# Two-layer decoder trunk on one core: an order from deadlines for four engines, and kept sums in 2 KB tiles

## The chip, the cores and the metric

The kernel runs on one core of a Trainium2 chip. A core has a matrix engine (PE, with its weight loads PEld), a vector engine (DVE), a scalar engine (ACT), GpSimd (POOL), and a queue processor (SP) that only issues transfers; ACT and POOL issue transfers too. Each engine works through its own list of instructions in the order in which they stand in the built program, and an instruction waits there on semaphores for what it needs. The metric is the device time of one execution in microseconds, as the median over several runs.

## The reference

The trunk has two layers over 256 positions and a model width of 2048, in float32, with a batch of one. Cut to what matters:

```python
h = rms_norm(x, mix_norm[l])
q, k, v, uv, gate_logits = split(h @ w_in[l])                 # 2048 x 7680
branch_a = sliding_window_attention(rope(norm(q)), rope(norm(k)), v, sinks[l]) @ w_attn_branch[l]
branch_b = chunked_sgu(gelu(uv), w_spatial[l], ...) @ w_sgu_branch[l]
gates = sigmoid(gate_logits)
merged = gates[..., :D] * branch_a + gates[..., D:] * branch_b
x = x + merged @ w_out[l]
h2 = rms_norm(x, ffn_norm[l])
x = x + (silu(h2 @ w_gate[l]) * (h2 @ w_up[l])) @ w_down[l]   # 2048 x 5632 and back
```

Attention has 16 query heads and 4 key heads of 64 and a window of 128; the gating unit mixes chunks of 128 positions in 8 groups. Nearly all the arithmetic is in the matrix products with the weights, which are read from HBM once.

## The kernel before

**Products.** Every weight matrix is cut into pieces of 256 rows by 512 columns (512 KB). Such a piece is an *entry*. It is loaded into a `raw` tile by a transfer on SP (L235), and split into a high part `whi` (a rounded copy on ACT, L261) and a low part `wlo` (`raw - whi` on DVE, L262). The activations are split in the same way into `uh` and `ul`. PE adds three products for each pair of blocks: `whi*uh`, `wlo*uh`, `whi*ul` (L361 and L362). An ordinary entry is 12 matmuls of 512 columns for both halves of the 256 positions.

Two column blocks that meet the same activations form a pair plan. In its head one or two units of four weight blocks are multiplied in Winograd's form with seven products in place of eight: DVE forms differences of weight blocks in place (L246), and of activation blocks (`sums`, `sh`, `sl`: L520 and L506, or L546 and L552 for a second unit). The head's entries, P1 to P7, are 6 matmuls each. ACT keeps one partial sum aside in `kept` (P5, L384), DVE adds to it (L387), and ACT writes it back into PSUM (L390). `kept` is one tile of 4 KB per partition from the pool `big` (31 slots).

**Order of PE.** PE's order is written out by hand: entries of a plan, with the head of the next plan woven into the end of the plan before. It is a manual schedule in both kernels.

**Order of the other engines.** The code asks for work at *slots*. A slot is passed each time an ordinary entry's worth of matmuls has been written, and `after(n, fn)` puts a step `n` slots ahead; `n` is a table of numbers set by hand (`WINO_NORM`, `SCORES`, `V_STEP` and so on, L28 to L58). Loads are asked for 7 entries ahead (`W_LOAD`), splits 4 ahead (`W_SPLIT`), weight differences 6 ahead (`W_SUM`). Steps are tied with `tc.issue_after` to the newest `wlo`, `whi` or load on their own engine, as here (L280 to L288):

```python
    def tick():
        slot_no[0] += 1
        due = [s for s in steps if s[0] <= slot_no[0]]
        steps[:] = [s for s in steps if s[0] > slot_no[0]]
        for _, fn in sorted(due, key=lambda s: s[0]):
            with tc.issue_after(stream.last.ins):
                fn()
```

The framework's scheduler then makes one list per engine from these ties and its own timeline.

**Pools.** `raw` tiles have 5 buffers, `whi` and `wlo` 4 each, `tmp` (tag `t2`, 2 KB per partition) 4, PSUM accumulators 4 and two times 2 smaller sets. `tmp` holds squares, attention scores (`pr`) and spatial weights. A feed-forward layer runs in three rounds of 4, 4 and 3 column blocks of 512. After each of the first two, `chunk` (L961 to L965) copies each result from PSUM into a 4 KB tile `part` of `big` and adds it to `held_x` in DRAM by one accumulating transfer of 512 KB from POOL. Transposes go through DVE (`box`, L431) and 16 transfers of 32 KB each (`gather`, L437), on SP, POOL or both.

Of the kernel before, what the change touches and what calls it, by code (L numbers as in the profile page):

```python
# [1 line left out]

# [6 lines left out]
F32 = mybir.dt.float32  # L9
# [3 lines left out]
AX = mybir.AxisListType  # L13

# [47 lines left out]

@with_exitstack
def hybrid_trunk(ctx: ExitStack, tc: tile.TileContext, x, mix_norm, w_in, q_norm, k_norm, sinks,
# [155 lines left out]
    class Stream:  # L220
# [7 lines left out]
        def load(self, upto):  # L228
            while self.asked < min(upto, len(entries)):
                for key, w, h, tag in entries[self.asked]["loads"]:  # L230
                    raw = (slot([P, 2, CW], name="raw") if tag == "slot" else
                           wraw.tile([P, 2, CW], F32, tag=tag, name=nm("raw"), bufs=None if tag == "raw" else 1))
                    for dst, src in rows_of(raw, w, h):
                        if self.raws:
                            self.loaded = nc.sync.dma_start(dst, src)  # L235
                        else:
                            for i in range(2):
                                self.loaded = nc.sync.dma_start(dst[:, i:i + 1], src[:, i:i + 1])
# [3 lines left out]
        def add(self, upto):  # L242
            while self.summed < min(upto, len(entries)):
                for d, x, y in entries[self.summed].get("sums", ()):
                    with tc.issue_after(self.last.ins):
                        self.last = nc.vector.tensor_tensor(out=self.raws[d], in0=self.raws[x], in1=self.raws[y],  # L246
                                                            op=ALU.subtract)
                self.summed += 1

        def split(self, upto):  # L250
            while len(self.parts) < min(upto, len(entries)):
# [5 lines left out]
                for i in ([slice(0, 1), slice(1, 2)] if one else [slice(0, 2)]):  # L257
                    if not self.parts and i.start == 0:
                        nc.vector.tensor_copy(hi[:, i, :], raw[:, i, :])
                    else:  # L260
                        self.high = nc.scalar.activation(hi[:, i, :], raw[:, i, :], AF.Copy)  # L261
                    self.last = nc.vector.tensor_tensor(out=lo[:, i, :], in0=raw[:, i, :], in1=hi[:, i, :].bitcast(F32),  # L262
                                            op=ALU.subtract)
# [18 lines left out]
    def tick():  # L282
# [38 lines left out]
    held = const.tile([P, 1], F32, name="held")  # L321
    hold = nc.gpsimd.tensor_copy(held, xs[2][:, 1, :1])

    def later(dst, src):
        with tc.issue_after(hold.ins):
            nc.gpsimd.dma_start(dst, src)
# [37 lines left out]
    def step():  # L364
# [17 lines left out]
        elif tag == "P5":  # L382
            p.kept = slot([P, 2, CW], name="kept")
            nc.scalar.activation(p.kept[:, 1, :], a[0], AF.Copy)  # L384
            nc.scalar.activation(a[0], a[1], AF.Copy)
        elif tag in ("P6", "P7"):
            nc.vector.tensor_tensor(out=p.kept[:, int(tag == "P7"), :], in0=a[1], in1=p.kept[:, 1, :], op=ALU.add)  # L387
        if "then" in e:
            for t, ps in enumerate(banks(p, "b")):
                nc.scalar.activation(ps, p.kept[:, t, :], AF.Copy)  # L390
# [208 lines left out]
    def squared(c):  # L599
        with tc.issue_after(stream.high.ins):  # L600
            norm.squares(c)

    for c in range(NCH):
        after(3 + c, lambda c=c: squared(c))
# [41 lines left out]
    class Layer:  # L646
# [493 lines left out]
```

## Time and profile before

| | |
|---|---|
| median of 3 runs | 2420.3 us (2419.92 to 2421.76) |
| span of the profiled execution, first to last instruction | 2416.4 us |
| the profiled execution's own time | not recorded; the median is 3.9 us over its span |
| busy: PE, PEld, DVE, ACT, POOL | 2405.1, 1970.7, 2092.0, 1532.4, 303.4 us |
| granted TensorE clock, mean | 1.000 |
| HBM read and written | 483.66 and 16.78 MB |
| transfer queues of SP and POOL | 63.6% and 6.2% of 16 engines' span |

The page of the profile lists busy time per engine, busy share in 40 slices, transfer queues, the chain of work that ended last, and the costliest groups of instructions. A line in a group or a timeline reads: line, engine, operation, tile written `<-` tiles read, shape, count, and in brackets the idle time of the engine just before, with what ended it. Matmuls overlap: each shows about 0.39 us, but they start 0.227 us apart when nothing is late.

### The profile page before, as it was taken

The numbers are of one execution on the slowest core, as the hardware profiler recorded it, in microseconds if no ns is written. First come the engines' busy times: TensorE is split into PE (matmuls) and PEld (weight loads), VectorE is DVE, ScalarE is ACT, GpSimd is POOL, SyncE is SP. The second block draws the span as 40 slices with busy tenths as digits, with TensorE's granted clock in tenths as the row PEclk, the third lists the DMA queues.
The fourth block names the chain that finished last, engine by engine and source line by source line (L and its number), as shares of the span: only waits on it lengthen the run. The fifth ranks groups of instructions, "written<-read, shape, count | busy, mean of one in ns | idle before, by whom it ended". The sixth has DMA issues, their size and how long they took to land.

```text
span 2416.4 us, 31069 instructions
## 1 busy us (share of the span) xinstructions
PE 2405.1 (100%) x10692; PEld 1970.7 (82%) x10692; DVE 2092.0 (87%) x2409; ACT 1532.4 (63%) x1932; POOL 303.4 (13%) x557
## 2 busy tenths in 40 slices
PE   9999999999999999999999999999999999999999
PEld 7877888888888888888888778888888888888887
DVE  7779787898999998799887897878889989998998
ACT  6477555576666675666665775555676666666665
POOL 1100001132110111001301000011311101110010
PEclk9999999999999999999999999999999999999999
DMA  8755678687677757776957557776867786677773
GB/s 287 233 167 164 178 204 251 221 264 239 191 238 228 239 179 223 245 225 178 293 177 260 174 160 197 215 223 227 269 219 232 213 258 204 199 231 229 235 223 138
DMA packets 285070, 527.16 MB, mean 218 GB/s; under 512 B 28208, under 2 KB 40080, under 8 KB 284912
## 3 DMA queue, kind: packets, MB, share of 16 engines
q1 hardware_dynamic: 263056, 486.36, 63.6%
q0 software_dynamic: 21536, 38.56, 6.2%
q8 instruction: 83, 1.36, 0.2%
q14 instruction: 75, 0.61, 0.1%
q10 hardware_dynamic: 320, 0.27, 0.0%
HBM read 483.66 MB, written 16.78 MB: 207 GB/s over the span
## 4 chain that ended last, share of the span: by engine, by line
PE 88%; DVE 4%; DMA 4%; issue 1%; ACT 1%; SPq 1%; POOL 0%; DVEq 0%; ACTq 0%
PE acc L361 58%; PE acc L362 29%; DVE wlo L262 2%; DMA raw<-in_w_up_dram 2%; DMA raw<-in_w_in_dram 1%; DMA tt<-box 1%; ACT whi L261 1%; DVE raw L246 1%; SPq L437 1%; PE psc L807 1%; PE po L859 0%; PE psg L942 0%; PE ppt L844 0%; PE pt L474 0%; POOL tt L437 0%
## 5 line engine op out<-in xcount | busy, mean ns | idle before, releaser
L261 ACT ACTIVATE whi<-raw 128x1024 fp32r<-128x1024 f32 (+1 forms) x1116 | 1166.6, 1058 | 786.3 <-PE acc L362 440.0
L262 DVE TENSOR_TENSOR wlo<-raw,whi 128x1024 fp32r<-128x1024 f32 (+1 forms) x1117 | 1343.5, 1216 | 269.3 <-ACT whi L261 255.3
L361 PE MATMUL acc<-whi,uh 128*128 128x512 f32 x2854 | 1116.7, 391 | 1.4 <-ACT uh L460 1.4
L361 PE MATMUL acc<-wlo,uh 128*128 128x512 f32 x2854 | 1113.3, 390 | 2.1 <-DVE wlo L262 1.3
L362 PE MATMUL acc<-whi,ul 128*128 128x512 f32 x2854 | 1112.1, 390 | 0.6 <-DVE ul L465 0.6
L361 PEld LDWEIGHTS acc<-wlo,uh 128*128 128x128 f32 x2854 | 536.0, 188 | 118.5 <-DVE wlo L262 6.6
L361 PEld LDWEIGHTS acc<-whi,uh 128*128 128x128 f32 x2854 | 535.9, 188 | 117.8 <-issue 4.9
L362 PEld LDWEIGHTS acc<-whi,ul 128*128 128x128 f32 x2854 | 535.9, 188 | 112.8 <-DVE ul L465 1.5
L437 POOL DMA_DIRECT2D tt<-box x464 | 228.0, 499 | 1202.6 <-DVE box L431 339.7
L246 DVE TENSOR_TENSOR raw<-raw,raw 128x1024 f32<-128x1024 f32 x292 | 355.5, 1218 | 5.2 <-DMA raw<-in_w_up_dram 2.9
L361 PE MATMUL acc<-wlo,sh 128*128 128x512 f32 x584 | 228.1, 391 | 2.0 <-DVE wlo L262 2.0
L361 PE MATMUL acc<-whi,sh 128*128 128x512 f32 x584 | 228.4, 391 | 0.0
L362 PE MATMUL acc<-whi,sl 128*128 128x512 f32 x584 | 227.5, 390 | 0.0
L361 PEld LDWEIGHTS acc<-wlo,sh 128*128 128x128 f32 x584 | 109.7, 188 | 26.3 <-DVE wlo L262 4.1
L361 PEld LDWEIGHTS acc<-whi,sh 128*128 128x128 f32 x584 | 109.7, 188 | 25.1 <-issue 2.3
L362 PEld LDWEIGHTS acc<-whi,sl 128*128 128x128 f32 x584 | 109.6, 188 | 22.7
L387 DVE TENSOR_TENSOR kept<-acc,kept 128x512 f32<-128x512 f32 x102 | 69.6, 682 | 9.3 <-PE acc L362 9.3
L390 ACT ACTIVATE acc<-kept 128x512 f32<-128x512 f32 x102 | 59.7, 588 | 2.3 <-DVE kept L387 1.0
L964 POOL DMA_DIRECT2D held_x<-part x16 | 13.9, 868 | 301.4 <-ACT part L963 301.4
L333 POOL TENSOR_TENSOR rv<-ve,neg_half 128x4 f32<-128x4 f32 x8 | 10.2, 1273 | 266.8 <-DVE ve L907 247.9
L384 ACT ACTIVATE kept<-acc 128x512 f32<-128x512 f32 x51 | 30.1, 591 | 10.8 <-PE acc L362 10.5
L829 ACT ACTIVATE pr<-pr,negm 128x128 f32<-128x128 f32 x64 | 24.9, 390 | 16.0 <-DVE negm L820 16.0
(149 smaller groups left out, 909.0 us busy)
## 6 DMA issues: line engine op xcount, KB each, us to landing
raw<-in_w_in_dram SPq DMA_DIRECT2D x239, 512.0 KB, 4.8
raw<-in_w_gate_dram SPq DMA_DIRECT2D x176, 512.0 KB, 4.6
raw<-in_w_up_dram SPq DMA_DIRECT2D x176, 512.0 KB, 5.4
raw<-in_w_down_dram SPq DMA_DIRECT2D x176, 512.0 KB, 5.3
raw<-in_w_out_dram SPq DMA_DIRECT2D x64, 512.0 KB, 6.9
raw<-in_w_attn_branch_dram SPq DMA_DIRECT2D x64, 256.0 KB, 7.0
raw<-in_w_sgu_branch_dram SPq DMA_DIRECT2D x32, 512.0 KB, 5.8
tt<-box POOLq DMA_DIRECT2D x464, 32.0 KB, 4.7
```

What stands on the lines that cost most here:

```text
L246: self.last = nc.vector.tensor_tensor(out=self.raws[d], in0=self.raws[x], in1=self.raws[y], op=ALU.subtract)
L261: self.high = nc.scalar.activation(hi[:, i, :], raw[:, i, :], AF.Copy)
L262: self.last = nc.vector.tensor_tensor(out=lo[:, i, :], in0=raw[:, i, :], in1=hi[:, i, :].bitcast(F32), op=ALU.subtract)
L361: nc.tensor.matmul(ps, a, part[:, kk, :], start=first and kk + n == 0, stop=False, skip_group_check=True)
L362: nc.tensor.matmul(ps, b, hi[:, kk, :], start=False, stop=kk == 1, skip_group_check=True)
L384: nc.scalar.activation(p.kept[:, 1, :], a[0], AF.Copy)
L387: nc.vector.tensor_tensor(out=p.kept[:, int(tag == "P7"), :], in0=a[1], in1=p.kept[:, 1, :], op=ALU.add)
L390: nc.scalar.activation(ps, p.kept[:, t, :], AF.Copy)
L437: q.dma_start(dst[j * B:(j + 1) * B, i], box[i * B:(i + 1) * B, j])
L807: nc.tensor.matmul(pscore[:, i, :nk], self.qT[pair // 4][j * HD:(j + 1) * HD, pair % 4, t * P:(t + 1) * P], self.kT[j * HD:(j + 1) * HD, : ...
L829: self.exps = nc.scalar.activation(pr4[:, h, :], pr4[:, h, :], AF.Exp, bias=nm_[:, h:h + 1], accum_out=den[:, h:h + 1])
L964: nc.gpsimd.dma_start(held_x[j], part, accum_op=ALU.add)
```

## The change

**What it does.** All `tc.issue_after` ties go. While the program is traced, every pool notes which tile has which home (`Homes`). At the end `in_order` goes over the traced instructions:

1. `works` gives each instruction a price (`Work`: a pitch for its engine, and a time to its result), and finds what it needs, who needs it, and which buffers it takes.
2. `count_back` starts from PE, whose matmuls are laid end to end, and counts back for every other instruction the latest time at which it may start (`due`). Engines and the transfer engines are each taken as one server.
3. `play` goes forward: whenever an engine is free, it takes of the instructions that are ready, and whose buffers are free, the one with the earliest `due`; a function that needs another table on ACT counts as due 4000 ns later. PE keeps its order.
4. The resulting list of each of DVE, ACT, POOL and SP is fixed by an ordering tie from each instruction to the next.

The slots still decide what is traced when, and with it the order of PE's few other matmuls. Apart from the order, two tiles change: `kept` becomes two 2 KB tiles of `tmp` (except in the `in` plans), and `part` becomes one 2 KB tile of `tmp` per half, each added to DRAM by an accumulating transfer of 256 KB. No arithmetic is added or dropped: PE has the same 10582 instructions and DVE the same 2411; POOL issues 32 accumulating transfers for 16; ACT loads a table 14 times for 10 (Exp 5 times for 3, Gelu 6 for 4).

**What moves, at three places.** The first is VectorE near 890 us, in the first layer's feed-forward part, where a plan with two Winograd units follows another. `raw<-raw` is a difference of weight blocks, `sums` and `sl` are activation differences for a plan some ten entries later. Before:

```order
L520 TENSOR_TENSOR sums_7836<-flat_7658 128x256
L262 TENSOR_TENSOR wlo_7842<-raw_7689,whi_7841 128x1024
L520 TENSOR_TENSOR sums_7836<-sums_7836,flat_7658 128x256
L262 TENSOR_TENSOR wlo_7852<-raw_7709,whi_7851 128x1024
L520 TENSOR_TENSOR sums_7836<-flat_7658 128x256
L520 TENSOR_TENSOR sums_7836<-flat_7658,sums_7836 128x256
L262 TENSOR_TENSOR wlo_7870<-raw_7447,whi_7869 128x1024
L246 TENSOR_TENSOR raw_7689<-raw_7761,raw_7689 128x1024
L262 TENSOR_TENSOR wlo_7885<-raw_7839,whi_7884 128x1024
L246 TENSOR_TENSOR raw_7709<-raw_7798,raw_7709 128x1024
L506 TENSOR_TENSOR sl_7881<-sums_7836,sh_7880 128x1024
L262 TENSOR_TENSOR wlo_7896<-raw_7689,whi_7895 128x1024
```

And now (L521 is the old L262, L506 the old L246):

```order
L521 TENSOR_TENSOR wlo_7863<-raw_7710,whi_7862 128x1024
L521 TENSOR_TENSOR wlo_7873<-raw_7730,whi_7872 128x1024
L506 TENSOR_TENSOR raw_7730<-raw_7819,raw_7730 128x1024
L506 TENSOR_TENSOR raw_7732<-raw_7819,raw_7732 128x1024
L521 TENSOR_TENSOR wlo_7891<-raw_7467,whi_7890 128x1024
L506 TENSOR_TENSOR raw_7710<-raw_7782,raw_7710 128x1024
L521 TENSOR_TENSOR wlo_7906<-raw_7860,whi_7905 128x1024
L506 TENSOR_TENSOR raw_7712<-raw_7782,raw_7712 128x1024
L521 TENSOR_TENSOR wlo_7917<-raw_7710,whi_7916 128x1024
L521 TENSOR_TENSOR wlo_7933<-raw_7730,whi_7932 128x1024
```

The four `sums` and `sl` have left this stretch: they now stand among the `wlo` of the following ten entries. The last `wlo` before (`wlo_7896`) is the last but one now (`wlo_7917`).

The second place is the queue of SP near 1257 us, at the start of the second layer: `kT` is the transposed key tile, `ln` a table for the gating unit. Before:

```order
L235 DMA raw_11029<-in_w_in_dram 128x2x512
L235 DMA raw_11060<-in_w_in_dram 128x2x512
L437 DMA kT_10831<-box_10967 32x256 x16
L669 DMA ln_11047<-in_sgu_ln_b_dram 128x1024
L235 DMA raw_11089<-in_w_in_dram 128x2x512
L235 DMA raw_11101<-in_w_in_dram 128x2x512
L235 DMA raw_11120<-in_w_in_dram 128x2x512
```

And now (L697 is the old L437, L496 the old L235):

```order
L496 DMA raw_11097<-in_w_in_dram 128x2x512
L697 DMA kT_10868<-box_11004 32x256
L924 DMA ln_11084<-in_sgu_ln_b_dram 128x1024
L697 DMA kT_10868<-box_11004 32x256 x3
L496 DMA raw_11126<-in_w_in_dram 128x2x512
L697 DMA kT_10868<-box_11004 32x256 x5
L496 DMA raw_11138<-in_w_in_dram 128x2x512
L697 DMA kT_10868<-box_11004 32x256
L496 DMA raw_11157<-in_w_in_dram 128x2x512
L697 DMA kT_10868<-box_11004 32x256 x3
L496 DMA raw_11184<-in_w_in_dram 128x2x512
L697 DMA kT_10868<-box_11004 32x256 x3
```

The 16 small transfers stood in one block; now four weight loads stand between them.

The third place is VectorE near 2366 us, in the head of the last residual; `pt` is a transposed activation block in PSUM. Before:

```order
L262 TENSOR_TENSOR wlo_20446<-raw_20392,whi_20445 128x1024
L246 TENSOR_TENSOR raw_20356<-raw_20358,raw_20356 128x1024
L552 TENSOR_TENSOR sl_20424<-sums_20323,sh_20423 128x1024
L262 TENSOR_TENSOR wlo_20487<-raw_20230,whi_20486 128x1024
L246 TENSOR_TENSOR raw_20372<-raw_20374,raw_20372 128x1024
L457 TENSOR_TENSOR ul_20467<-pt_20468,uh_20466 128x512
L457 TENSOR_TENSOR ul_20467<-pt_20475,uh_20466 128x512
L262 TENSOR_TENSOR wlo_20502<-raw_20356,whi_20501 128x1024
```

And now (L812 is the old L552, L717 the old L457):

```order
L521 TENSOR_TENSOR wlo_20519<-raw_20465,whi_20518 128x1024
L506 TENSOR_TENSOR raw_20445<-raw_20447,raw_20445 128x1024
L521 TENSOR_TENSOR wlo_20560<-raw_20302,whi_20559 128x1024
L812 TENSOR_TENSOR sl_20497<-sums_20396,sh_20496 128x1024
L521 TENSOR_TENSOR wlo_20575<-raw_20429,whi_20574 128x1024
L521 TENSOR_TENSOR wlo_20587<-raw_20445,whi_20586 128x1024
L717 TENSOR_TENSOR ul_20540<-pt_20541,uh_20539 128x512
L717 TENSOR_TENSOR ul_20540<-pt_20548,uh_20539 128x512
```

Both `ul` now stand behind two more `wlo`, and one weight difference stands ahead of this piece. At the very start, VectorE copied `first_cols` (L316) behind the cast of the first weights (L259); now the copy stands first.

**The diff,** cut to its core:

```diff
+HAND = {PE: 54, DVE: 40, ACT: 40, POOL: 80, SP: 30}
+COST_PE = {"psg": 500, "po": 450, "psc": 400}
+SWITCH = 4000
+LATE = 0
+EARLY = 40000
+SPARE = 30000
...
+class Work:
...
+        if self.engine == PE:
+            n = elements(ins.ins[0].ap[1:])
+            self.pitch = 227 if n == CW and out.startswith("acc") else COST_PE.get(out.split("_")[0], 110)
+            self.time = 390
+        elif op == "DMACopy":
...
+            serve = size / row * (9 + row * 75 / 2048) / 16
...
+            if "cce_op=AluOpType.add" in str(ins):
+                serve *= 2
+            self.dma = serve, (2200 if far else 1550) + (900 if self.engine == POOL and size > 40000 else 0)
+            self.pitch = {SP: 648, POOL: 505}.get(self.engine, 60)
+            self.time = sum(self.dma) + 50
+        elif self.engine == ACT:
+            self.pitch = 105 + n * 0.8335 + (60 if min(sizes) == 1 else 0)
+            self.time = self.pitch + 98
+        elif self.engine == DVE:
+            self.pitch = 68 + n / 0.96 + (25 if op == "StreamTranspose" else 60 if op == "TensorScalarPtr" and n == P else 0)
+            self.time = self.pitch + 81
...
+def count_back(todo):
+    at, by = 8000.0, []
+    for w in todo:
+        if w.engine == PE:
+            w.due, at = at, at + w.pitch
+        by.append(at + SPARE)
...
+    def latest(w):
+        t = w.due + w.time if w.engine == PE else by[w.k]
+        for k in w.users + w.reused:
+            t = min(t, todo[k].due - HAND[todo[k].engine])
+        for k in w.ahead:
+            t = min(t, todo[k].due + w.time)
+        return t
...
+        if w.dma:
+            t = min(-t - 50, free.get("dma", end))
+            free["dma"] = t - w.dma[0]
+            w.due = free[w.engine] = min(t - sum(w.dma), free.get(w.engine, end) - w.pitch)
+        elif w.engine != PE:
+            w.due = free[w.engine] = min(-t - w.time + w.pitch, free.get(w.engine, end)) - w.pitch
...
+def play(todo, users, homes):
...
+            ks = [k for k in waiting[e] if ready[k] <= t and (e != PE or k == turn[0]) and fits(todo[k])]
+            if not ks:
+                continue
+            w = todo[min(ks, key=lambda k: (todo[k].due + (SWITCH if todo[k].table not in (None, table) else 0), k))]
...
+            if w.dma:
+                served = max(served, at + w.dma[1]) + w.dma[0]
+                end = served + 50
+            order[e].append(w)
...
+def in_order(tc, homes, held):
+    todo, users = works(tc.nc.cur_bb.bb.instructions, homes, held)
+    count_back(todo)
+    queued = mybir.DependencyInfo(mybir.DependencyClass.NoSync, mybir.DependencyReason.DATA)
+    order = play(todo, users, homes)
+    for e in (DVE, ACT, POOL, SP):
+        for a, b in zip(order[e], order[e][1:]):
+            tc.add_manual_dep(b.ins, a.ins.name, queued, reason="in_order")
...
         for _, fn in sorted(due, key=lambda s: s[0]):
-            with tc.issue_after(stream.last.ins):
-                fn()
+            fn()
...
         elif tag == "P5":
-            p.kept = slot([P, 2, CW], name="kept")
-            nc.scalar.activation(p.kept[:, 1, :], a[0], AF.Copy)
+            if p.key[0] == "in":
+                whole = slot([P, 2, CW], name="kept")
+                p.kept = [whole[:, i, :] for i in range(2)]
+            else:
+                p.kept = [temp(name="kept") for _ in range(2)]
+            nc.scalar.activation(p.kept[1], a[0], AF.Copy)
...
             if j not in xt:
-                part = slot([P, NT, CW], name="part")
                 for t in range(NT):
-                    nc.scalar.activation(part[:, t, :], sums[t], AF.Copy)
-                nc.gpsimd.dma_start(held_x[j], part, accum_op=ALU.add)
+                    part = temp(name="part")
+                    nc.scalar.activation(part, sums[t], AF.Copy)
+                    nc.gpsimd.dma_start(held_x[j][:, t, :], part, accum_op=ALU.add)
                 return
```

More of the change, by code (lines that the diff above doesn't have):

```diff
@@ L1 @@
+from collections import deque
 from contextlib import ExitStack
+from heapq import heappop, heappush
 import concourse.bass as bass
@@ new lines, in elements, with region, overlap @@
+def elements(ap):
+    n = 1
+    for _, c in ap:
+        n *= c
+    return n
+def region(a):
+    ap, off, name = a.ap, 0, str(getattr(a, "memref", ""))
+    if getattr(a, "bass_ap", None) is not None:
+        name, off, ap = a.bass_ap.tensor.name, a.bass_ap.offset, a.bass_ap.ap
+    step = ap[0][0]
+    p, lo = (off // step, off % step) if step else (0, off)
+    return name, (p, p + ap[0][1], lo, lo + sum(s * (c - 1) for s, c in ap[1:]) + 1)
+def overlap(a, b):
+    return a[0] < b[1] and b[0] < a[1] and a[2] < b[3] and b[2] < a[3]
@@ new lines, in works, with covers @@
+def works(traced, homes, held):
+    def covers(b, x):
+        return b[0] <= x[0] and b[1] >= x[1] and b[2] <= x[2] and b[3] >= x[3]
+    todo, users, wrote, read, last = [], {}, {}, {}, {}
+    for ins in traced:
+        if ins.engine not in ENGINES or ins.opcode in ("TilePoolBoundary", "TileManualSchedule", "RegisterMove"):
+            continue
+        w = Work(len(todo), ins)
+        todo.append(w)
+        for name, b in w.operands + w.outs:
+            w.deps |= {k for k, x in wrote.get(name, ()) if overlap(b, x)}
+        for name, b in w.outs:
+            w.deps |= {k for k, x in read.get(name, ()) if overlap(b, x)}
+            if w.engine in (DVE, ACT) and (name, w.engine) in last:
+                w.deps.add(last[name, w.engine])
+        for name, b in w.outs:
+            last[name, w.engine] = w.k
+            wrote[name] = [x for x in wrote.get(name, ()) if not covers(b, x[1])] + [(w.k, b)]
+            read[name] = [x for x in read.get(name, ()) if not overlap(b, x[1])]
+        for name, b in w.operands:
+            read.setdefault(name, []).append((w.k, b))
+        for name in {name for name, _ in w.operands + w.outs if name in homes}:
+            users.setdefault(name, []).append(w.k)
+        w.deps = {k for k in w.deps if k != w.k}
+    at = {w.ins.name: w.k for w in todo}
+    for first, then in held:
+        todo[at[first.name]].ahead.add(at[then.name])
+    takers = {}
+    for name, ks in users.items():
+        todo[ks[0]].takes.append(name)
+        todo[ks[0]].ahead.update(ks[1:])
+        takers.setdefault(homes[name], []).append((ks[0], name))
+    for (_, bufs, cyclic), rows in takers.items():
+        rows.sort()
+        order = list(dict.fromkeys(k for k, _ in rows))
+        if bufs < len(rows):
+            for a, b in zip(order, order[1:]):
+                todo[a].ahead.add(b)
+        if cyclic:
+            for (_, old), (k, _) in zip(rows, rows[bufs:]):
+                todo[k].reuse |= {u for u in users[old] if u < k}
+    for w in todo:
+        w.ahead = {k for k in w.ahead if w.k not in todo[k].deps}
+        for k in w.ahead:
+            todo[k].behind.add(w.k)
+    for w in todo:
+        w.reuse -= w.deps | w.behind
+        for k in w.deps:
+            todo[k].users.append(w.k)
+        for k in w.reuse:
+            todo[k].reused.append(w.k)
+    return todo, users
```

189 lines of the change are left out of this document (137 added, 52 removed).

## The prediction

> **What bounds the kernel now.** I read the page's head first, then the groups of PE, then stretches of the span, and last the timeline where a stretch has idle PE.
>
> ```profile
> span 2416.4 us, 31069 instructions
> PE 2405.1 (100%) x10692; PEld 1970.7 (82%) x10692; DVE 2092.0 (87%) x2409; ACT 1532.4 (63%) x1932; POOL 303.4 (13%) x557
> ...
> L361 PE MATMUL acc<-wlo,uh 128*128 128x512 f32 x2854 | 1113.3, 390 | 2.1 <-DVE wlo L262 1.3 <-DVE kept L387 0.3
> L362 PE MATMUL acc<-whi,ul 128*128 128x512 f32 x2854 | 1112.1, 390 | 0.6 <-DVE ul L465 0.6
> ...
> L361 PE MATMUL acc<-wlo,sh 128*128 128x512 f32 x584 | 228.1, 391 | 2.0 <-DVE wlo L262 2.0
> ```
>
> PE is the bound: it is idle for only 11.3 us. The change leaves PE's list alone, so all that it can win is time in which PE waits. The groups show whom it waits for: nearly always DVE, for a `wlo` that comes late. The stretches show where (columns: length, then busy time and count for PE, PEld, DVE, ACT, POOL, then clock, transfer share and GB/s):
>
> ```profile
> 0.00:40.00 40.00, 36.25 (x169) 29.74 (x170) 27.79 (x76) 26.86 (x51) 9.57 (x24) 1.00 0.95 326
> 830.00:930.00 100.00, 99.46 (x437) 81.35 (x436) 95.57 (x95) 65.84 (x75) 22.95 (x47) 1.00 0.66 203
> 1140.00:1220.00 80.00, 79.70 (x356) 64.69 (x355) 67.93 (x84) 55.26 (x82) 20.14 (x40) 1.00 0.86 278
> 1220.00:1310.00 90.00, 89.32 (x398) 73.81 (x397) 72.23 (x89) 49.07 (x54) 12.37 (x7) 1.00 0.65 210
> 2035.00:2130.00 95.00, 94.46 (x415) 77.17 (x414) 92.01 (x94) 61.84 (x71) 20.69 (x43) 1.00 0.65 202
> 2130.00:2335.00 205.00, 204.94 (x904) 169.47 (x903) 185.89 (x176) 134.36 (x152) 22.05 (x42) 1.00 0.72 224
> 2335.00:2372.00 37.00, 35.45 (x160) 28.81 (x159) 35.14 (x38) 23.98 (x30) 2.15 (x4) 1.00 0.77 271
> 2372.00:2417.00 45.00, 40.47 (x179) 33.02 (x177) 34.03 (x37) 20.32 (x22) 0.00 (x0) 0.99 0.32 106
> ```
>
> 3.75 us of idle PE lie in the first 40 us. The last stretch lacks 4.5 us, of which 0.6 lie past the span's end and 3.9 are the last result's way out, behind the last matmul; no order changes that. In between six stretches lack 0.54, 0.30, 0.68, 0.54, 0.06 and 1.55, together 3.67 us. 3.75 + 3.9 + 3.67 is all of the 11.3, so PE is not idle anywhere else. In two of them DVE is busy for 96% and 97% of the time, in a third for 95%.
>
> A stall costs more than the idle time shown:
>
> ```profile
> 2367.14 0.39 PE L361 MATMUL acc<-whi,sh 128*128 128x512 f32 x1
> 2368.78 0.50 PE L361 MATMUL acc<-wlo,sh 128*128 128x512 f32 x1 [1.25 <-DVE wlo L262]
> 2369.12 0.39 PE L362 MATMUL acc<-whi,sl 128*128 128x512 f32 x1
> 2369.35 0.40 PE L361 MATMUL acc<-whi,sh 128*128 128x512 f32 x1
> ```
>
> Undelayed matmuls start 0.23 us apart (2369.12 to 2369.35). Here three starts take 1.64 and 0.34 us, 1.52 more than twice 0.23, for 1.25 idle: 0.27 on top. With that surcharge per stall, and the stalls that I count in the timeline of each stretch (3, 4, 1, 3, 1, 2), there are 1.35, 1.4, 0.95, 1.35, 0.3 and 2.1 us to win, 7.4 together. That is an estimate, and 7.4 plus a part of the start's is the ceiling of this change.
>
> **Two backlogs of DVE (830 to 930, 2035 to 2130).**
>
> ```profile
> 887.29 0.42 DVE L520 TENSOR_TENSOR sums<-flat 128x256 f32<-128x256 f32 x1
> 887.63 0.42 DVE L520 TENSOR_TENSOR sums<-flat,sums 128x256 f32<-128x256 f32 x1
> ...
> 892.50 1.22 DVE L506 TENSOR_TENSOR sl<-sums,sh 128x1024 fp32r<-128x1024 f32 x1
> 893.64 3.49 DVE L262 TENSOR_TENSOR wlo<-raw,whi 128x1024 fp32r<-128x1024 f32 x3
> ```
>
> A full-width DVE instruction takes 1.14 us start to start (892.50 to 893.64), a quarter-width one 0.34, and nothing is idle between them: PE waits since DVE has too much ahead of `wlo`. Between two given `wlo` five entries apart, the old order has five `wlo`, three weight differences, `sl` and four `sums`; the new has five `wlo` and four differences. The count of full-width ones is equal; the four quarter-width `sums` go (4 x 0.34 = 1.4 us). One entry earlier the old order has a weight difference more, 1.1. So the late `wlo` comes 2.5 us sooner, against 1.35 us of stall: all of it goes, in both layers, **2.7**. What moved back, `sums` and `sl`, now stands beside ordinary entries, whose 12 matmuls take 12 x 0.227 = 2.7 us of PE for 1.14 of DVE; that is its cover. Without it, it would cost its own 2.5 again.
>
> **The block of small transfers on SP (1220 to 1310).**
>
> ```profile
> 1256.52 0.37 SPq L235 DMA_DIRECT2D raw<-in_w_in_dram  x1
> 1257.19 11.12 SPq L437 DMA_DIRECT2D kT<-box  x16
> ...
> 1269.04 1.40 SPq L235 DMA_DIRECT2D raw<-in_w_in_dram  x3
> ...
> 1307.59 0.50 PE L361 MATMUL acc<-wlo,uh 128*128 128x512 f32 x1 [0.68 <-DVE wlo L262]
> ```
>
> From 1256.5 to 1269.0 no weight load is issued, as 16 key transfers of about 0.63 us each and one wait stand in a block. The loads behind bunch up, and PE pays at 1307.6. With four weight loads among the 16, the longest gap is five transfers, about 3.2 us. The stall goes: **1.0**. The keys themselves come later by four issues, 4 x 0.4 = 1.6 us; PE's list reads them first behind the matmul at 1307.6, some 40 us after the last was issued (1268.3).
>
> **The last residual's head (2335 to 2372).** Ahead of the `wlo` that stalls by 1.25 us the old piece holds three full-width instructions besides two `wlo`, and two half-width `ul` (0.6 each, half of 1.14): 5 x 1.14 + 2 x 0.6 = 6.9 us. The new one, from the `wlo` that answers to its first, has `wlo`, `sl`, `wlo` and one difference less: 3 x 1.14 = 3.4, of which 1.14 was only moved ahead. Net 2.3 us sooner against 1.5 of stall. The stall before it (0.3 idle, for `kept`) gains less; I take **1.9** of 2.1, bounds 1.0 and 2.1.
>
> **The start.**
>
> ```profile
> 6.85 0.43 DVE L259 CAST whi<-raw 128x512 fp32r<-128x512 f32 x1 [5.77 <-DMA raw<-in_w_in_dram]
> 7.19 0.17 DVE L316 COPY first_cols<-pf 128x16 f32<-128x16 f32 x1
> ...
> 8.33 1.13 DVE L465 SCALAR_TENSOR_TENSOR ul<-pt,first_cols,uh 128x128 fp32r<-128x128 f32 x4 [0.33 <-ACT uh L460]
> 9.37 0.68 DVE L262 TENSOR_TENSOR wlo<-raw,whi 128x512 fp32r<-128x512 f32 x1
> ...
> 5.05 1.57 PE L474 MATMUL pt<-ident,x 128*128 128x128 f32 x8
> 7.98 0.50 PE L361 MATMUL acc<-whi,uh 128*128 128x512 f32 x1 [1.35 <-ACT uh L460]
> ```
>
> The copy waits behind a cast that waits for weights until 6.85, and ACT's `uh` waits for the copy. In front of the cast the copy runs at about 5.2, `uh` when `pt` is done (6.5), and the first matmul when the cast is (7.3): 0.6 sooner; and the second `wlo` stands behind two of the four `ul` (1.04 us for four), 0.5 more. The third wait there, 0.6 for `ul` (first fence), follows DVE's and ACT's backlog and I leave it. **1.0**, bounds 0 and 1.9.
>
> **The other two stretches.** For 1140 to 1220 (transposes and four reloads of `x` at the round's end) the order shows one reload earlier and no clear relief: **0.6**, bounds 0 and 1.4. For 2130 to 2335, **0.1** of 0.3.
>
> **Added work.** `kept` and `part` in 2 KB tiles do no work more on ACT. POOL issues 16 transfers more:
>
> ```profile
> L964 POOL DMA_DIRECT2D held_x<-part x16 | 13.9, 868 | 301.4 <-ACT part L963 301.4
> SPq L235 <- DMA held_x<-part: 11.5, 3, 4.7
> held_x<-part POOLq DMA_DIRECT2D x16, 512.0 KB, 8.0
> raw<-in_w_in_dram SPq DMA_DIRECT2D x239, 512.0 KB, 4.8
> raw<-in_w_out_dram SPq DMA_DIRECT2D x64, 512.0 KB, 6.9
> L829 ACT ACT_TABLE_LOAD x3 | 3.8, 1283 | 0.1
> ACT whi L261 <- PE acc L362: 440.0, 440, 3.2
> ```
>
> 16 x 0.87 = 14 us on an engine that is 13% busy: nothing; its idle time covers it, and without that each would delay a `tt` gather by 0.87. The 31 larger slots get room: loads waited three times, 11.5 us in all, for a `part` to leave. PE is idle in no stretch with such transfers but 2130 to 2335, by 0.06, so that is worth nothing by itself. Four more table loads are 4 x 1.28 = 5.1 us of ACT, which waits 440 us for PE to free `whi` buffers (last row): hidden, 5.1 if not.
>
> [...]
>
> **The sum.** 2.7 + 1.0 + 1.9 + 1.0 + 0.6 + 0.1 = 7.3 to win. Against it I set 1.0 for new stalls (bounds 0 and 7.4, next part). Net 6.3. The durations are from one execution with a span of 2416.4, which becomes 2410.1; the median lies 3.9 above that span, so 2420.3 - 6.3 = **2414.0**.
>
> **The rivals.**
>
> *Loads just in time by too short a price.* The new order takes a weight load to land 2200 + 256 rows x 84 / 16 + 50 = 3.6 us after its issue, with no reserve (`LATE = 0`). The rows above say 4.8 in the middle, and 6.9 for `w_out`. Where it places a load or a tail of differences to be just in time, it is 1.2 us late and PE pays 1.5 with the surcharge. For it: the weight blocks of a coming head are now loaded behind ordinary loads that they preceded. Against it: ordinary loads are still issued as buffers come free, and 51 heads each have several entries of reserve. If one head in ten pays, that is 5 x 1.5 = 7.4, and the time is 2420.4: no change.
>
> *Every stall goes and none comes.* 7.4 + 1.9 = 9.3, hence 2411.0. Against it: 1140 to 1220 has stalls of three different causes.
>
> Two chunks of one pair follow each other like this:
>
> ```profile
> 742.25 0.92 POOL L964 DMA_DIRECT2D held_x<-part  x1 [25.56 <-ACT part L963]
> 750.40 0.88 POOL L964 DMA_DIRECT2D held_x<-part  x1 [7.23 <-ACT part L963]
> ```
>
> *Slower: the four tiles of `tmp`.* In the residual of a round the next plan's `kept` holds two of them and the first chunk's `part` two, until its transfers land. If the two halves land one after the other at the 8.0 us that 512 KB took, the second tile is free after 16, while the second chunk follows by 8.2 us (750.40 - 742.25); by the program four of the eight pairs are that close. ACT then stands 8 us with all splits behind it. Beyond the 3.2 us that it was ahead at most, PE pays 4.8 each, 19 in all: 2413.0 (no other new stall) + 19 = 2432. It decides from a landing of 8 + 3.2 = 11.2 us on. Against it: halves of 256 KB should not take as long as the whole each.
>
> *Table loads on the path.* All four: 2414.0 + 5.1 = 2419.1, no change that can be told. [...]
>
> That the change doesn't do what it says is excluded by the order shown: the lists did move.
>
> **How the numbers follow.** 0.2% of 2420.3 is 4.8 us, about what a measurement of this kernel tells from no change, so faster means below 2415.5. My forecast, 2412 to 2415.4, has 0.45; all stalls gone, 0.15; late loads 0.25; table loads 0.08; `tmp` 0.07. Faster is 0.45 + 0.15 = 0.60, the same 0.25 + 0.08 = 0.33, slower 0.07. The range goes from just under the ceiling's 2411.0 through the late loads' 2420.4: 2410.7 to 2421.0.
>
> **What would show it.** Right: between 830 and 930, 1220 and 1310, 2035 and 2130, and 2335 and 2372 PE is idle by 0.1 at most; the first `acc` matmul starts near 7.4; no gap of 12 us between weight loads near 1257; the whole idle time of PE is 7 or less. Wrong: ACT's `part` or `kept` groups with idle time released by `held_x` (the `tmp` rival), PE idle by `raw` transfers in heads (late loads), or the same DVE stalls at the same places.

## The result, and the profile after

| | before | after |
|---|---|---|
| median of 4 runs each | 2420.1 us (2417.4 to 2421.8) | 2453.2 us (2451.4 to 2458.2) |
| ratio, 95% interval | | 1.0142 (1.0128 to 1.0157) |
| span of the profiled execution | 2416.4 us | 2449.7 us (its own time 2451.4) |

The change makes the kernel 33 us slower. The forecast was 6 us faster, with a range up to 2421.0. Head and PE groups of the page of after (L617 and L618 are the old L361 and L362, L647 the old L387):

```profile
span 2449.7 us, 31107 instructions
PE 2417.1 (99%) x10692; PEld 1973.3 (81%) x10692; DVE 2106.4 (86%) x2409; ACT 1543.6 (63%) x1936; POOL 319.3 (13%) x573
...
L617 PE MATMUL acc<-wlo,uh 128*128 128x512 f32 x2854 | 1116.9, 391 | 17.5 <-DVE kept L647 11.0
```

PE is still the bound, but it is now idle for 32.6 us (2449.7 - 2417.1) where it was 11.3, and its busy time grew by 12 us with the same 10692 matmuls. The largest releaser is new: `kept`, an addition of 0.7 us on DVE, ended 11.0 us of PE's idle time; before, it was 0.3.

PE's list is the same in both kernels, so the start of the same matmul can be compared in the two traces. By how much each stretch is longer than before (boundaries at times of the kernel before, us; the last stretch ends at the start of the last matmul; the last column is a kernel of the experiments below):

```
stretch of before      after   prices 5500 and 4400
   0 to   40           +1.67        +0.99
  40 to  400           +0.10        +1.39
 400 to  480           +1.62        -0.05
 480 to  560          +11.69         0.00
 560 to  640           -0.05        -0.05
 640 to  700           +1.74        +0.09
 700 to  760           +2.14        +0.38
 760 to  830           -0.22        -0.12
 830 to  930           -0.76        -0.17
 930 to 1140           +0.54        -0.17
1140 to 1220           +1.30        -1.67
1220 to 1310           -0.99        -0.99
1310 to 1600           -0.16        -0.16
1600 to 1680           +1.83        -0.07
1680 to 1780           +9.64         0.00
1780 to 1900           +0.30        +0.09
1900 to 2035           +2.13        +0.48
2035 to 2130           -0.77        -0.11
2130 to 2335           +2.93        -0.27
2335 to 2372           -1.63        -2.13
2372 to the end        -0.10        -0.07
sum                   +32.96        -2.60
```

Two thirds of the loss (11.69 + 9.64) lie in two stretches for which the prediction had no term: the end of the residual after the mixing part, in each layer, where the normed activations are transposed by `box` and the gathers `tt<-box` for the first feed-forward plans. The timelines of after at the first of them, of POOL, ACT, DVE and PE (L697 issues the gather, L720 reads it, L725 reads `uh` as well):

```profile
529.37 3.94 POOL L697 DMA_DIRECT2D tt<-box  x8 [5.57 <-DVE box L691]
534.87 3.92 POOL L697 DMA_DIRECT2D tt<-box  x8 [1.56 <-DMA tt<-box]
...
543.64 1.30 ACT L720 ACTIVATE uh<-tt,vcols 128x256 fp32r<-128x256 f32 x3 [5.71 <-DMA tt<-box]
544.85 1.04 ACT L520 ACTIVATE whi<-raw 128x1024 fp32r<-128x1024 f32 x1
...
537.21 2.35 DVE L521 TENSOR_TENSOR wlo<-raw,whi 128x1024 fp32r<-128x1024 f32 x2
544.18 1.67 DVE L725 SCALAR_TENSOR_TENSOR ul<-tt,vcols,uh 128x128 fp32r<-128x128 f32 x6 [4.62 <-ACT uh L720]
545.76 0.68 DVE L647 TENSOR_TENSOR kept<-acc,kept 128x512 f32<-128x512 f32 x1
...
541.61 0.39 PE L618 MATMUL acc<-whi,ul 128*128 128x512 f32 x1
546.50 0.80 PE L617 MATMUL acc<-wlo,uh 128*128 128x512 f32 x1 [4.50 <-DVE kept L647]
547.10 0.63 PE L617 MATMUL acc<-whi,uh 128*128 128x512 f32 x1
547.52 0.63 PE L618 MATMUL acc<-whi,ul 128*128 128x512 f32 x1
```

Read it from below. PE waits 4.5 us for `kept`. `kept` stands in DVE's list behind six `ul`, which wait for `uh` from ACT; ACT's `uh` waits 5.71 us for transfers, the last of which POOL issued at 538.3 (end of its last row less one issue of 0.5). `uh` started at 543.6, 5.3 us later. `kept` itself lacked nothing, and a `whi` behind `uh` on ACT lacked nothing either: they stood in a queue. Then PE runs 13 matmuls 0.43 us apart (547.10 to 547.52) in place of 0.23. The second layer has the same chain (ACT, then PE):

```profile
1761.00 1.31 ACT L720 ACTIVATE uh<-tt,vcols 128x256 fp32r<-128x256 f32 x3 [4.61 <-DMA tt<-box]
...
1763.86 0.50 PE L617 MATMUL acc<-wlo,uh 128*128 128x512 f32 x1 [3.45 <-DVE kept L647]
```

The kernel before at the same place: the gather is issued in one go, and its reader on ACT comes 11 us after the last issue and waits for nothing.

```profile
520.86 7.83 POOL L437 DMA_DIRECT2D tt<-box  x16 [6.61 <-DVE box L431]
...
539.67 1.70 ACT L460 ACTIVATE uh<-tt,vcols 128x256 fp32r<-128x256 f32 x4
```

The waits of ACT for gathers over the whole span (us in total, times, longest), after and then before:

```profile
ACT uh L716 <- DMA tt<-box: 27.8, 9, 5.8
ACT uh L720 <- DMA tt<-box: 27.5, 6, 6.9
ACT flat L761 <- DMA tt<-box: 22.0, 5, 6.9
ACT qT L1045 <- DMA tt<-box: 11.5, 4, 5.4
```

```profile
ACT qT L791 <- DMA tt<-box: 14.7, 4, 5.8
ACT uh L456 <- DMA tt<-box: 2.1, 2, 1.7
```

88.8 us against 16.8 in these rows. What a gather costs, and what the planner thinks, differ. The gathers that POOL issues in after, with the median from issue to landing:

```profile
tt<-box POOLq DMA_DIRECT2D x464, 32.0 KB, 4.7
```

The planner takes 32 rows of 1 KB at 46.5 ns, over 16 engines, 93 ns; with its fixed 1550 and 50 that is 1.7 us, 3.0 too short. The price isn't far from what a gather took while fewer other transfers ran. The gather of the kernel before above (520 to 529 us, DMA share 0.46) and that of after (529 to 539, DMA share 0.78), median from issue to landing:

```profile
tt<-box POOLq DMA_DIRECT2D x16, 32.0 KB, 1.7
```

```profile
tt<-box POOLq DMA_DIRECT2D x16, 32.0 KB, 4.3
```

### The profile page after: what moved, and what is told of

It is laid out like the page before. It is cut to its first block, busy times and chain, and to the rows that moved or that the text cites. A ratio compares the mean times of both kernels' runs of the same rounds, so it can differ in the third digit from the quotient of the medians.

```text
span 2449.7 us, 31107 instructions
## 1 busy us (share of the span) xinstructions
PE 2417.1 (99%) x10692; PEld 1973.3 (81%) x10692; DVE 2106.4 (86%) x2409; ACT 1543.6 (63%) x1936; POOL 319.3 (13%) x573
## 4 chain that ended last, share of the span: by engine, by line
PE 56%; DVE 7%; DMA 6%; issue 3%; ACT 1%; POOL 1%; SPq 0%; ACTq 0%; DVEq 0%; POOLq 0%
PE acc L617 37%; PE acc L618 18%; DVE wlo L521 4%; DMA tt<-box 2%; DMA raw<-in_w_down_dram 2%; ACT whi L520 1%; DVE raw L506 1%; DMA raw<-in_w_up_dram 1%; POOL tt L697 1%; DMA raw<-in_w_out_dram 0%; DMA held_x<-part 0%; DVE box L691 0%; PE psc L1061 0%; DVE hid L1327 0%; DMA held_x<-x 0%
## 5 line engine op out<-in xcount | busy, mean ns | idle before, releaser
L521 DVE TENSOR_TENSOR wlo<-raw,whi 128x1024 fp32r<-128x1024 f32 (+1 forms) x1117 | 1337.9, 1217 | 241.7 <-ACT whi L520 234.9
L617 PE MATMUL acc<-wlo,uh 128*128 128x512 f32 x2854 | 1116.9, 391 | 17.5 <-DVE kept L647 11.0
L617 PE MATMUL acc<-whi,uh 128*128 128x512 f32 x2854 | 1118.9, 392 | 0.1
L618 PE MATMUL acc<-whi,ul 128*128 128x512 f32 x2854 | 1113.7, 390 | 0.0
L617 PEld LDWEIGHTS acc<-wlo,uh 128*128 128x128 f32 x2854 | 537.2, 188 | 140.2 <-DVE wlo L521 15.4
L617 PEld LDWEIGHTS acc<-whi,uh 128*128 128x128 f32 x2854 | 537.3, 188 | 117.5 <-issue 3.4
L618 PEld LDWEIGHTS acc<-whi,ul 128*128 128x128 f32 x2854 | 537.2, 188 | 112.5 <-DVE ul L725 0.8
L697 POOL DMA_DIRECT2D tt<-box x464 | 228.9, 500 | 1207.4 <-DVE box L691 456.0
L506 DVE TENSOR_TENSOR raw<-raw,raw 128x1024 f32<-128x1024 f32 x292 | 355.2, 1222 | 21.5 <-DMA raw<-in_w_up_dram 8.6
L617 PE MATMUL acc<-wlo,sh 128*128 128x512 f32 x584 | 228.4, 391 | 4.7 <-DVE wlo L521 4.7
L617 PE MATMUL acc<-whi,sh 128*128 128x512 f32 x584 | 228.4, 391 | 1.4 <-ACT acc L645 1.4
L618 PE MATMUL acc<-whi,sl 128*128 128x512 f32 x584 | 227.4, 389 | 0.0
L617 PEld LDWEIGHTS acc<-wlo,sh 128*128 128x128 f32 x584 | 109.6, 188 | 30.3 <-DVE wlo L521 7.4
L617 PEld LDWEIGHTS acc<-whi,sh 128*128 128x128 f32 x584 | 109.6, 188 | 26.5 <-ACT acc L645 1.8
L618 PEld LDWEIGHTS acc<-whi,sl 128*128 128x128 f32 x584 | 109.6, 188 | 22.7
L647 DVE TENSOR_TENSOR kept<-acc,kept 128x512 f32<-128x512 f32 x102 | 69.7, 683 | 1.2 <-PE acc L618 1.2
L1212 POOL DMA_DIRECT2D held_x<-part x32 | 27.5, 858 | 294.4 <-ACT part L1211 294.4
L716 ACT ACTIVATE uh<-tt 128x512 fp32r<-128x512 f32 x42 | 24.8, 624 | 39.8 <-DMA tt<-box 27.8
L717 DVE TENSOR_TENSOR ul<-tt,uh 128x512 fp32r<-128x512 f32 x42 | 27.8, 687 | 23.3 <-ACT uh L716 20.9
```

Source lines behind the costliest of these rows:

```text
L617: nc.tensor.matmul(ps, a, part[:, kk, :], start=first and kk + n == 0, stop=False, skip_group_check=True)
L618: nc.tensor.matmul(ps, b, hi[:, kk, :], start=False, stop=kk == 1, skip_group_check=True)
L647: nc.vector.tensor_tensor(out=p.kept[int(tag == "P7")], in0=a[1], in1=p.kept[1], op=ALU.add)
L697: q.dma_start(dst[j * B:(j + 1) * B, i], box[i * B:(i + 1) * B, j])
L716: nc.scalar.activation(h, s_, AF.Copy)
L717: nc.vector.tensor_tensor(out=l, in0=s_, in1=h.bitcast(F32), op=ALU.subtract)
```

## The experiments

Two theories stood at the start. **A**: the computed lists are at fault, since the planner's price for a gather is too short and readers stand in ACT's and DVE's lists before their data are there. **B**: the pools are, since `kept`, `part` and the squares share four tiles of `tmp`. Every kernel here computes the same thing; ratios are to the kernel before, run on the same chip in the same series.

### One part of the change at a time

The changed kernel with the 4 KB tiles of before:

```diff
-                p.kept = [temp(name="kept") for _ in range(2)]
+            whole = slot([P, 2, CW], name="kept")
+            p.kept = [whole[:, i, :] for i in range(2)]
...
-                    part = temp(name="part")
+                part = slot([P, NT, CW], name="part")
```

> The changed kernel, but `kept` and `part` stand in the 4 KB pool as before; the computed order stays. Theory A (the order: ScalarE's list puts readers of `tt` where the planner takes a transfer of 32 KB to land 1.7 us after its issue, the trace shows 4.7, and the splits behind them stand still): still slow, 2443 to 2460 us, with over 60 us of idle ScalarE that ends with a `tt` transfer. Theory B (the four tiles of `tmp`, shared by `kept`, `part`, squares): back to 2415 to 2425 us.

Measured: 2455.7 us, ratio 1.0149 (1.0129 to 1.0168). ACT waits 80.3 us for gathers. The order alone makes the whole loss; B falls. (Its trace, of an execution of 2461 us, loses 15.6 us in the two stretches above and 5.5 to 6.6 in each of three others, at 760, 1140 and 1900, that grew by 2.1 at most in after: where the stalls fall changes with the lists.)

The other part alone: the kernel before, with the same lines the other way round.

> The kernel before, with `kept` and `part` in the 2 KB pool as in the change, and the old order by hand-set slots. Theory A: within 5 us of the kernel before, 2415 to 2425. Theory B: slow, 2440 to 2455.

Measured: 2425.2 us, ratio 1.0024 (1.0014 to 1.0033). Just past the 5 us that A allowed: some 6 us. In its trace the growth is spread (1.2 us at the start, where the first product even came earlier and the matmuls then ran at half pace; 1.1 between 760 and 830, 1.3 between 2210 and 2270, 2.9 in the last residual's head, where a late `wlo` made PE wait 1.8 us and then run slowly). ACT's own waits for `part` to leave are small:

```profile
ACT part L967 <- DMA held_x<-part: 3.2, 3, 1.9
```

Why they add up to 6 us stays open.

### The price of a gather

One number:

```diff
-            self.dma = serve, (2200 if far else 1550) + ...
+            self.dma = serve, (2200 if far else 4700) + ...
```

> The changed kernel with one number changed: the fixed part of the planner's price for a transfer from SBUF to SBUF is 4700 ns in place of 1550. Theory A: the stalls of PE that follow on ScalarE's waits for `tt` go, which are about 22 us (11.7 between 490 and 555 us, 1.6 at 666, 9 between 1710 and 1770, the stretches at a slower clock included): 2431 us, range 2425 to 2437; ScalarE's idle time that ends with a `tt` transfer falls from 89 us to under 30. Theory B: no change, 2450 to 2456.

Measured: 2423.5 us, ratio 1.0015 (1.0005 to 1.0025): 30 us of the 33 are gone, below A's range (2425 to 2437) and more than the 22 that were attributed to the gathers by following single stalls. ACT's waits for gathers are halved, to 45.5 us:

```profile
ACT uh L720 <- DMA tt<-box: 22.2, 6, 4.6
...
ACT uh L716 <- DMA tt<-box: 10.8, 6, 2.6
...
ACT flat L761 <- DMA tt<-box: 7.9, 3, 4.0
...
ACT qT L1045 <- DMA tt<-box: 4.6, 2, 2.3
```

Under 30 was expected. So time and waits do not fall together, and A as it stood was not the whole of it.

Half the step, 3100 in place of 1550:

> The changed kernel with the price between SBUF and SBUF at half of the step, 3100 ns. Theory A: between the two ends measured (2453 at 1550, 2423.5 at 4700), about in the middle, 2432 to 2444 us, and ScalarE's idle time by `tt` transfers between 89 us and 45. If the gain of the run with 4700 came from a list that happened to fall well, this one may lie anywhere, above 2453 too.

Measured: 2436.4 us, ratio 1.0065 (1.0051 to 1.0079), in the middle, with 67.0 us of waits. The price works by degrees, which speaks against a list that fell well by chance.

### The price of the other transfers

Both raised, 6300 and 3700:

> The changed kernel with both fixed parts raised: 6300 ns in place of 1550 between SBUF and SBUF (GpSimd also stands 2 us for older transfers in a gather, which the planner does not know), 3700 in place of 2200 from or to HBM. Theory A: as the run with the gather's price, and the stalls by late weight differences (741, 1955, 2250 us: 2.1 + 1.5 + 1.6) go as well: 2426 us, range 2418 to 2433. Theory B: 2450 to 2456. If loads that are priced longer come too early instead and take `raw` buffers away, it is above the run with the gather's price alone.

Measured: 2421.6 us, ratio 1.0008 (0.9999 to 1.0017). Of the stalls by late weight differences at 741, 1955 and 2250 under 0.1 us each is left. Two new ones came, of 1.8 us of idle time each, at 897 and 2098. The timeline of DVE ahead of the first:

```profile
891.92 0.42 DVE L780 TENSOR_TENSOR sums<-flat 128x256 f32<-128x256 f32 x1
...
894.86 1.22 DVE L766 TENSOR_TENSOR sl<-sums,sh 128x1024 fp32r<-128x1024 f32 x1
896.00 2.35 DVE L521 TENSOR_TENSOR wlo<-raw,whi 128x1024 fp32r<-128x1024 f32 x2
```

It is the backlog that the change had moved away: with a gather priced at 6.4 us, 1.7 over the median, `sums` and `sl` stand in front of the `wlo` of a head again. The stretch 830 to 930 goes with the price of the gather: 0.78 us shorter than before at 4700, 0.17 at 5500, 2.81 longer at 6300. A price can be too long as well.

Only the loads and reloads, 3700 with 1550 for the gathers:

> The changed kernel with only the other price changed: 3700 ns in place of 2200 for a transfer from or to HBM, 1550 between SBUF and SBUF as in the change. Theory A (the price of the gathers is the cause): the waits of ScalarE for `tt` stay, over 60 us, and the time stays at 2440 us or more. Theory C (any price that is too short makes a list without reserve; priced longer, the loads and reloads leave ScalarE further ahead, so that its waits for `tt` no longer reach PE): 2422 to 2435 us, with the waits for `tt` still long but PE idle by under 15 us.

Measured: 2422.5 us, ratio 1.0008 (0.9999 to 1.0017). The gathers are priced as short as in the change, and still all but some 2 us of the loss is gone: theory C, not A alone. ACT's waits for gathers are 50.7 us, and PE is idle for 13.4 us. POOL, ACT and DVE at the place of the worst stall:

```profile
527.78 3.91 POOL L697 DMA_DIRECT2D tt<-box  x8 [1.44 <-DMA tt<-box]
...
535.92 0.51 ACT L720 ACTIVATE uh<-tt,vcols 128x256 fp32r<-128x256 f32 x1 [3.67 <-DMA tt<-box]
...
533.64 0.68 DVE L647 TENSOR_TENSOR kept<-acc,kept 128x512 f32<-128x512 f32 x1
537.41 1.23 DVE L521 TENSOR_TENSOR wlo<-raw,whi 128x1024 fp32r<-128x1024 f32 x1 [3.09 <-ACT whi L520]
```

ACT still waits 3.67 us for the gather. But DVE has done `kept` before it comes to anything that needs `uh`, and PE goes on. So here the wait for a transfer costs PE nothing by itself; it costs what stands behind it in the two lists and is due soon.

### Prices near what the rows show

> Both prices near the landings in the trace: 4700 and 3700 (256 rows of 84/16 ns come on top of the latter: 5.0 us; the trace has 4.6 to 6.0). Theory A: the stalls that were left in the run with 4700 and 2200 (566 us: 1.1, 773: 0.6, 1769: 1.8, 1976: 0.9, 2224: 0.8, and the slow start, some 3) lose their cause, and the backlog at 897 and 2098 us of the run with 6300 and 3700 (2.1 each and about 1.5 at the slower clock behind it) does not come: 2414 to 2419 us, at or below the kernel before.

Measured: 2417.6 us, ratio 0.9986 (0.9977 to 0.9996).

> Prices some 0.8 us over the middle landing, 5500 and 4400, for transfers that land later than the median (up to 7 us for `w_out`). If late single transfers make the stalls that are left, it is 1 to 3 us below the run with 4700 and 3700; if pricing them longer pushes other work back (`sums` and `sl` of a late gather ahead of a `wlo`, as at 897 us with 6300), 1 to 4 us above it.

Measured: 2415.5 us, ratio 0.9977 (0.9968 to 0.9986): 38 us faster than the change as it stood, and faster than the kernel before. Two of PE's groups in its trace:

```profile
L617 PE MATMUL acc<-wlo,uh 128*128 128x512 f32 x2854 | 1112.3, 390 | 1.4 <-DVE kept L647 1.1 <-DVE wlo L521 0.2
...
L617 PE MATMUL acc<-wlo,sh 128*128 128x512 f32 x584 | 228.2, 391 | 2.1 <-DVE wlo L521 1.9
```

> A try for the fastest: 5100 between SBUF and SBUF (the backlog at 897 and 2098 us was 2.1 us at 6300, 1.1 at 5500 and 0.3 to 0.4 at 4700 and below), 5200 from or to HBM. Theory A with a reserve for late loads: 2412 to 2416 us. If the higher price of loads costs buffers, 2416 to 2420.

Measured: 2417.1 us, ratio 0.9990 (0.9981 to 0.9999), not the 2412 to 2416 that was tried for. The backlog is smaller (the two stretches at 830 and 2035 take 0.63 less than before, in place of 0.17 and 0.11), but a stretch between 640 and 700 takes 4.2 us more. Among these three the best can't be told for certain: the intervals touch.

### Which half of the price matters

The prices enter twice: when due times are counted back, and when the lists are made forward. The function `price` adds 3950 and 2200 to the fixed parts in between:

```diff
     count_back(todo)
+    price(todo, 3950, 2200)
     ...
     order = play(todo, users, homes)
```

> The prices 5500 and 4400 hold only while the lists are made forward (when a transfer's reader counts as ready); the due times are counted back with the change's own 1550 and 2200. If what went wrong is that a list puts a reader where its data are not there yet (theory A, with C: for every kind of transfer), this is as good as both together: 2413 to 2419 us. If the due times were at fault (transfers asked for too late), 2435 to 2453.

Measured: 2416.1 us, ratio 0.9989 (0.9980 to 0.9998). And with the longer prices only while due times are counted:

> The other half: due times counted back with 5500 and 4400, lists made forward with the change's 1550 and 2200. Theory A: the readers stand in the lists as early as in the change, so it stays slow, 2440 to 2460 us, with over 60 us of idle ScalarE that ends with a `tt` transfer. If the due times were at fault: 2413 to 2425.

Measured: 2450.7 us, ratio 1.0126 (1.0109 to 1.0142). The waits of ACT for gathers, first of the run with long prices in the forward pass, then of the other:

```profile
ACT uh L725 <- DMA tt<-box: 7.6, 8, 1.8
...
ACT flat L770 <- DMA tt<-box: 2.3, 2, 1.2
```

```profile
ACT uh L730 <- DMA tt<-box: 28.0, 6, 6.6
ACT uh L726 <- DMA tt<-box: 22.8, 8, 4.4
...
ACT flat L771 <- DMA tt<-box: 12.1, 4, 4.9
ACT qT L1055 <- DMA tt<-box: 10.6, 4, 5.2
```

The forward pass decides; the due times were good enough. It takes an instruction when it believes its data to be there, and fixes that place for good; where it believes so too early, an engine that could have worked stands still.

### The pools, under good lists

> The prices 5500 and 4400, with `kept` and `part` in the 4 KB pool as before the change. The pools' part of the change by itself, under lists that are right: with the short prices it was 2455.7 against 2453.2, within the spread, and with the old lists it cost 6. If the 2 KB tiles leave loads and gathers room, this is 2 to 6 us above 2415.5; if they only bring their own waits, 1 to 5 us below.

Measured: 2420.4 us, ratio 1.0007 (0.9999 to 1.0016), against 0.9977 (0.9968 to 0.9986) with the 2 KB tiles. By the ratios, from two chips, the tiles are worth 0.3%, 7 us, when the lists are right; by the medians and the two traces 4.9 us; against the run with the prices in the forward pass alone, on the same chip, 4.3. With the old lists, which were set by hand for the old tiles, they cost 0.2%. In the traces most of the difference lies in four stretches: 1.7 us between 1900 and 2035, 1.3 between 2270 and 2335, 0.8 between 1140 and 1220, 0.6 between 700 and 760.

## Why the prediction was wrong

**The step that failed** is the term "minus 1.0 for new stalls (bounds 0 and 7.4)". In the trace of after the stretches that grew make 37.6 us together (the positive rows of the table). The bounds came from the rival of late loads: a price for weight loads that is 1.2 us too short, times one head in ten. The cause was of that kind (a price below the landing that the rows show, with no reserve), but the prediction weighed it for one sort of transfer and left out the gathers, whose price was 3.0 us under their median. Raising either price alone brought the time back to 2422 to 2424 us, so it is the missing reserve as a whole that cost, not the gather's price alone. And the prediction let a late transfer cost PE the lateness alone. In fact what was due behind the waiting reader on ACT and on DVE was late with it: `kept`, which lacked nothing, ended 4.50 us of idle PE at 546.5. It also left out that PE's next matmuls ran slowly behind so long a stall (13 of them 0.43 us apart there).

**The two backlogs of DVE: right in kind, too large.** 2.7 forecast; the stretches are 0.76 and 0.77 shorter, 1.5 together. 0.26 and 0.25 us of idle PE are left there, of 0.54 each. With the prices 5500 and 4400 only 0.3: the backlog partly returns.

**The block of small transfers on SP: right.** 1.0 forecast, 0.99 measured, in after and with good prices.

**The last residual's head: right.** 1.9 forecast, 1.63 in after; 2.13 with good prices, which is the upper bound given (2.1).

**The start: wrong sign in the trace, and not by idle time.** 1.0 faster forecast, 1.67 slower. The copy did run at 5.2, as said. But the forecast took `pt` as done at 6.5, and PE stood for `x` in the middle of it (DVE, PE and ACT in after):

```profile
5.16 0.17 DVE L573 COPY first_cols<-pf 128x16 f32<-128x16 f32 x1 [4.09 <-PE pf L571]
...
7.60 1.75 PE L734 MATMUL pt<-ident,x 128*128 128x128 f32 x7 [2.07 <-DMA x<-in_x_dram]
9.07 0.80 PE L617 MATMUL acc<-whi,uh 128*128 128x512 f32 x1
...
11.36 0.63 PE L617 MATMUL acc<-wlo,uh 128*128 128x512 f32 x1
11.79 0.63 PE L618 MATMUL acc<-whi,ul 128*128 128x512 f32 x1
...
8.54 0.47 ACT L720 ACTIVATE uh<-pt,first_cols 128x256 fp32r<-128x256 f32 x1 [5.78 <-PE pt L734]
```

PE waits 2.07 us for `x`, `uh` could start at 8.5 only, and the first product at 9.07. Over the stretch, though, PE is idle for 3.5 us in after and 3.75 before. What is longer is the matmuls: they start 0.43 us apart until 13 us (11.36 to 11.79), those of the kernel before 0.23 apart from 10.4 on. With 5500 and 4400 the first product started near the 7.3 of the forecast and PE is idle for 2.5 us only; its matmuls run at half pace to 12.9 us, and the start was 0.99 slower (PE there):

```profile
7.31 0.80 PE L617 MATMUL acc<-whi,uh 128*128 128x512 f32 x1
...
11.20 0.63 PE L617 MATMUL acc<-whi,uh 128*128 128x512 f32 x1
11.63 0.63 PE L617 MATMUL acc<-wlo,uh 128*128 128x512 f32 x1
```

With 6300 and 3700 PE is idle for 3.7 us, but its matmuls are at full pace, and the start is 0.55 faster than before (PE there):

```profile
10.51 0.39 PE L617 MATMUL acc<-whi,uh 128*128 128x512 f32 x1
10.74 0.40 PE L617 MATMUL acc<-wlo,uh 128*128 128x512 f32 x1
```

So the pace decides this stretch, and the prediction has no term for it. What sets it stays open: there is one trace of each kernel, and the kernel before with the 2 KB tiles, with the old lists, had half pace from 9.8 to 13.0 us as well.

**1140 to 1220, and 2130 to 2335.** 0.6 and 0.1 faster forecast, 1.30 and 2.93 slower in after; with good prices 1.67 and 0.27 faster, more than forecast. The gain was there and was buried under the new stalls.

**"Worth nothing by itself"**, said of the room that the 2 KB tiles give: wrong, 4 to 7 us with good lists.

**The rivals.** "Loads just in time" had the right kind of cause, at a fifth of its size. "`tmp`": ACT waited 1.5 us in all for `part` to land in after, and the run with the order alone excludes it. "Table loads": they are as many in the run at 2415.5 as in the change (14), and PE lost nothing to them that can be seen. "All stalls gone" was not reached by any run.

The forecast of 2414.0 is near what the change gives with prices a little over the rows (2415.5), but that is partly luck: there the two backlogs gave 0.3 in place of 2.7 and the start lost 0.99 in place of winning 1.0, while 1140 to 1220 won 1.67 in place of 0.6 and 40 to 400 lost 1.39 for which there was no term.

## What to carry to other kernels

Where a planner fixes the order of in-order engines, its price for a transfer is a promise to everything behind the reader: set it from the landing times in the trace, per kind of transfer and at or a little over the median while the other transfers run, before judging the order. Here two such numbers decide over 38 us, and with the better ones the computed lists beat those tuned by hand. When a forecast rests on such a planner, compare each of its prices with the row for it, and ask of each that is too short who stands behind the reader in the list.

## What the runs showed of the hardware

A stall of PE can cost more than its idle time and the 0.27 us of the prediction. Over the traces of both kernels and of eleven experiments, between 20 and 2385 us, stalls of 0.3 to 1.8 us were followed by matmuls at half pace (0.43 us apart) in 2 of 112 cases, both right behind another stall; stalls of 1.8 to 2.5 us in 7 of 12; longer ones (2.67 to 5.42 us) in all 5. In the traces of before and after alone, none of 21 stalls of 0.3 to 1.85 us was followed so, and both longer ones (3.45 and 4.50 us) were. Half pace lasted 6 to 13 matmuls, 1.2 to 2.6 us more. The granted clock shows it, here behind the stall of 4.50 us in the change (length, busy times, then clock):

```profile
545.69:552.52 6.83, 6.02 (x14) 4.76 (x15) 6.79 (x9) 5.41 (x10) 0.46 (x1) 0.50 0.50 152
```

A slow landing also slowed the issue of gathers. POOL issued eight transfers of 32 KB in 3.9 us and then stood about 1.5 us for an older one to land (1.56 and 1.44 in the rows `tt<-box x8` above); in after 47 such waits make 50.3 us. The semaphores in the trace of after show which one: POOL's 535 transfers use eight semaphores in turn, and none was issued before the transfer eight ahead of it had landed. The issue at 534.87 waited for the transfer issued at 529.37, which landed at 534.59. The wait stands in the program's instructions: 434 of the 535 issues name their own semaphore as one to wait for. In the row `x16` of the kernel before, with a median landing of 1.7 us, POOL issued 16 in one go. No price of the planner has these waits. Whether 5500 is better than the bare landing for that reason was not tested, and that it is better than 4700 is not certain.

```profile
POOL tt L697 <- DMA tt<-box: 50.3, 47, 2.1
```
